# An encoder trunk on one core: the opening stage loads its one-hot table first, moves the bias-line products and re-deals the modulation sums

## The chip, the core and the metric

The kernel runs on one NeuronCore of a Trainium2 chip. TensorE (PE, with its weight loads as PEld) does matrix products, VectorE (DVE), ScalarE (ACT) and GpSimd (POOL) the elementwise work, and SyncE (SP) issues most of the DMA transfers; ACT and POOL can issue transfers too. Each engine works through its own instruction list in order and waits on semaphores for the others. The metric is the device time of one execution in microseconds (us), the median over several executions.

## What is computed

Two transformer layers over 1024 tokens of width 1024, fp32. Layer 0 is a dilated-window attention with a T5 bias by relative position, layer 1 a latent attention. Each layer first forms `u = x*(1+scale)+shift`, with `shift` and `scale` made from a conditioning vector:

```python
for i in range(DEPTH):
    mod = jax.nn.silu(c) @ ada_w[i] + ada_b[i]
    shift, scale, gate = jnp.split(mod[:, None, :], 3, axis=-1)
    u = x * (1 + scale) + shift
    ...
    x = layernorm(DEEPNORM_ALPHA * x + gate * y, ln_g[i], ln_b[i])
# in layer 0, per head: s = q.k/8 + bias_table[t5_bucket(distance)] inside the window
```

Only the opening of layer 0 is touched: the modulation (shift and scale), the first three output blocks of the input projection (q, k and v of the first head pair), and the lines of bias that all heads of layer 0 read.

## The kernel before

`startup` is the opening stage. Its order is written out by hand: every engine gets its instructions in the order of the Python calls. The contraction over 1024 channels is cut into eight slices `dd` of 128. For each slice it loads 1 MB of modulation weights (two tiles `ada`) and 512 KB of transposed input (`xc`), forms two columns (shift and scale for 128 channels), forms `u`, and adds the slice's share to six PSUM banks `ip`, two halves of 512 tokens for each of three weight blocks `wa`.

- **The columns.** `mod_acc(dd)` (L205-216) lets VectorE add up `SHARE[dd]` of the eight 128x256 weight pieces into `acc`, each scaled by a column of `sc` (the silu of the conditioning vector). `mod_sums(dd)` (L218-227) has TensorE sum the other pieces and `acc` over the partitions, with products of a single column into the bank `pm`: two per piece, each shown as two instructions in the profile. `mod_col(dd)` (L229-234) adds the bias columns `bcol` on ScalarE.
- **u in two parts.** fp32 products are done as three fp32r products of high and low parts. `u_hi` (L236-245) makes the high part `uh` (and the exact value back into `xc`), `u_lo` (L247-248) the low part `ul`. `w_split` (L102-106) does the same for weights: `wh` on ScalarE, `wl` here on VectorE.
- **The block.** `in_block(dd)` (L254-269) has 18 products of 512 columns, six for each weight block: `uh,wh`, `uh,wl` and `ul,wh` for two halves.
- **Zeros.** `zeros(n)` (L163-165) issues n products of 512 columns on a tile of zeros into a bank that nobody reads. They only keep TensorE occupied.
- **The bias lines.** `bias_load` loads the 32x18 table (`rb`, whose padding POOL fills) and the one-hot table `oh` (33 rows of 6 KB). `bias_line(g)` multiplies them, one product per head group, and ScalarE copies six rows to `lines`; `bias_write` stores these in DRAM, where `bias_tile` reads them per head.

In what order: the first slice's sums run with zeros between them, then the first block with the second slice's sums woven into it. From then on slice `dd`'s sums are issued, then the whole block of slice `dd-1`, so that the columns, `uh` and `ul` of `dd` are made during that block. The line products stand after the block of slice 5 (one) and after that of slice 6 (two, written at the start of `layer_a_attention` and moved there by the scheduler, which orders what follows the hand-written part); they are `pl` in the profile. Loads go out on SP in the order of the calls; every load takes one of eight semaphores in turn and waits until the load that had that semaphore eight loads earlier has landed. After `startup` come the projections (`pj`), layer 0's attention, and the rest, none of which the diff changes apart from the two line products at the start of `layer_a_attention`.

Of the kernel before, what the change touches and what calls it, by code (L numbers as in the profile page):

```python
# [34 lines left out]
SHARE = (4, 3, 5, 7, 7, 7, 7, 7)  # L35


ZEROS = (10, 6)
# [31 lines left out]
class Trunk:  # L70
# [85 lines left out]
    def startup(self):  # L156
# [13 lines left out]
        nc.scalar.dma_start(self.bcol1, A["ada_b1"])  # L170
        nc.scalar.activation(self.sc, self.sc, AF.Silu)
        self.rb = KP.tile([33, P], F32, name="rb")
        nc.gpsimd.memset(self.rb, NEG)
# [9 lines left out]
        def load_x(dd):  # L183
            t = self.gt(F32, "xc")
            sync.dma_start(t, A["xt"][dd])
            return t
# [16 lines left out]
        acc_psum = [[self.bank("ip") for _ in range(2)] for _ in range(3)]  # L203
        accs, pms = {}, {}

        def mod_acc(dd):
            w = [adas[dd][k // 4][:, (k % 4) * 256 : (k % 4) * 256 + 256] for k in range(8)]
            n = SHARE[dd]
            parts = [(w[k], self.sc[:, k : k + 1]) for k in range(8 - n)]
            if n:  # L210
                a = KP.tile([P, 256], F32, tag="ot", bufs=3, name=self.nm("acc"))
                nc.vector.tensor_scalar(a, w[8 - n], self.sc[:, 8 - n : 9 - n], None, op0=ALU.mult)
                for k in range(9 - n, 8):
                    nc.vector.scalar_tensor_tensor(a, w[k], self.sc[:, k : k + 1], a, op0=ALU.mult, op1=ALU.add)
                parts.append((a, self.ones))
            accs[dd] = parts

        def mod_sums(dd):  # L218
# [3 lines left out]
            for j in range(2):  # L222
                for i, (w, x) in enumerate(parts):
                    nc.tensor.matmul(
                        pm[:, j : j + 1], w[:, j * P : j * P + P], x, start=i == 0, stop=i == len(parts) - 1
                    )
                    yield 1.0
# [26 lines left out]
        def in_block(dd, blocks=(0, 1, 2)):  # L254
            for b in blocks:
                h, l = whl[b]
                ks = slice(dd * P, dd * P + P)
                hh, hl, lh = (h, self.uh[dd]), (h, self.ul[dd]), (l, self.uh[dd])
                if dd or b:
                    todo = [(x, hf) for x in (hh, lh, hl) for hf in range(2)]  # L260
                else:
                    todo = [(hh, 0), (hl, 0), (hh, 1), (lh, 0), (lh, 1), (hl, 1)]
                seen = set()
                for n, ((w, u), hf) in enumerate(todo):
                    nc.tensor.matmul(  # L265
                        acc_psum[b][hf], w[:, ks], u[:, hf * 512 : hf * 512 + 512],
                        start=dd == 0 and hf not in seen, stop=dd == NK - 1 and n >= 4,
                    )
                    seen.add(hf)
                    yield 1.0  # L270
# [17 lines left out]
        split(1)  # L288
        mod_acc(1)
        weave((in_block(0, (1,)), 6.0), (mod_sums(1), 12.0))  # L290
        split(2)
        for dd in range(1, NK):
            if dd + 2 < NK:
                load_d(dd + 2)
            if dd == 2:
# [1373 lines left out]
```

## Time and profile before

| | |
|---|---|
| timed runs, median of 3 | 1365.49 us (1363.44 to 1368.98) |
| the profiled execution | 1372.24 us, its span 1370.4 us |
| TensorE busy | 1339.2 us (98% of the span) |
| VectorE, ScalarE, GpSimd busy | 855.7, 798.4, 562.5 us |
| opening stage, up to the first projection product | 69.04 us |
| DMA from 10 to 40 us | 400 GB/s, all 16 engines taken |
| mean granted TensorE clock over the span | 0.987 |

The span is the time from the first to the last instruction of one profiled execution; 1.84 us of its own time lie around it. A view of stretches gives the busy time of each engine in a stretch (with the number of instructions), the granted clock as a share of full speed, and what the DMA engines moved. The chain of waits is followed back from the last instruction: each row has a start, a length and the work that held up the end. Rows of the timeline have start, length, engine, line, what is written and read, and in brackets how long the engine stood idle before it and for whom.

### The profile page before, as it was taken

What the parts mean: (1) busy time and instruction counts of PE and PEld (TensorE: products, weight loads), DVE (VectorE), ACT (ScalarE), POOL (GpSimd) and SP (SyncE); (2) the same over time, 40 slices, a digit from 0 to 9 for tenths busy, and PEclk for the clock granted to TensorE, in tenths of its full rate; (3) what the DMA queues carried; (4) which work ended last, traced back from release to release, by engine and by line L of the source; (5) the groups of instructions that cost most, each with busy time, mean ns of one, the idle gap of its engine ahead of it and who ended that gap; (6) DMA issues with size and microseconds to landing.
All of it is one profiled execution on the core that took longest, in us unless ns stands there. A gap on an engine that the chain in (4) does not pass through costs nothing.

```text
span 1370.4 us, 20504 instructions
## 1 busy us (share of the span) xinstructions
PE 1339.2 (98%) x7464; PEld 1152.6 (84%) x7464; DVE 855.7 (62%) x1473; ACT 798.4 (58%) x1631; POOL 562.5 (41%) x550
## 2 busy tenths in 40 slices
PE   8999999999999999999999999999999999999997
PEld 7788888888888888888988888898889889898776
DVE  5554454445445344566734278887887887777887
ACT  3575555554443432355742288788788878887421
POOL 0142233123222266614632344744553473444761
PEclk6999999999999999999999999999999999999998
DMA  9422221113244254552154011111112111113322
GB/s 361 109 66 37 60 62 40 37 48 99 85 143 152 64 158 136 186 175 115 62 143 153 0 34 30 24 41 25 30 27 54 30 24 28 25 55 118 114 93 92
DMA packets 44980, 114.28 MB, mean 83 GB/s; under 512 B 6917, under 2 KB 13333, under 8 KB 44880
## 3 DMA queue, kind: packets, MB, share of 16 engines
q1 hardware_dynamic: 40184, 100.43, 24.0%
q0 software_dynamic: 4096, 12.24, 3.6%
q8 instruction: 59, 0.97, 0.3%
q14 instruction: 41, 0.34, 0.1%
q10 hardware_dynamic: 600, 0.32, 0.1%
HBM read 96.42 MB, written 8.67 MB: 77 GB/s over the span
## 4 chain that ended last, share of the span: by engine, by line
PE 73%; DVE 10%; ACT 7%; DMA 5%; issue 4%; SPq 0%; POOL 0%; DVEq 0%; ACTq 0%; POOLq 0%
PE pj L92 8%; PE pj L94 8%; PE pj L93 8%; PE o L1388 6%; PE t L1368 5%; PE s L92 3%; PE s L94 3%; PE s L93 3%; DMA ada<-ada_row 3%; PE ip L265 3%; PE po L92 2%; PE po L94 2%; PE po L93 2%; DVE mb L1328 2%; PE t L564 2%
## 5 line engine op out<-in xcount | busy, mean ns | idle before, releaser
L92 PE MATMUL pj<-uh,wh 128*128 128x512 f32 x528 | 217.5, 412 | 0.0
L94 PE MATMUL pj<-uh,wl 128*128 128x512 f32 x528 | 207.5, 393 | 0.0
L93 PE MATMUL pj<-ul,wh 128*128 128x512 f32 x528 | 207.3, 393 | 0.0
L1328 DVE TENSOR_REDUCE mb<-s 128x1 f32<-128x1024 f32 x128 | 155.6, 1216 | 48.8 <-PE s L94 47.9
L1372 DVE TENSOR_TENSOR ptl<-t,pth 128x512 fp32r<-128x512 f32 x256 | 165.0, 680 | 5.3 <-ACT pth L1371 3.2
L1371 ACT CAST pth<-t 128x512 fp32r<-128x512 f32 x256 | 139.4, 589 | 37.8 <-PE t L1368 34.4
L105 POOL TENSOR_TENSOR wl<-wraw,wh 128x1024 fp32r<-128x1024 f32 x42 | 106.2, 2533 | 123.0 <-ACT wh L104 93.2
L1336 ACT ACTIVATE pr<-s,mb 128x1024 f32<-128x1024 f32 x128 | 144.2, 1126 | 15.1 <-DVE mb L1328 14.5
L1368 PEld LDWEIGHTS t<-ident,pr 128*128 128x128 f32 x1024 | 119.3, 141 | 19.0 <-DVE ptl L1372 2.8
L1368 PE MATMUL t<-ident,pr 128*128 128x128 f32 x1024 | 133.0, 272 | 2.1 <-DVE ptl L1372 2.1
L1388 PE MATMUL o<-pth,vq 128*128 128x256 f32 x512 | 130.4, 292 | 1.1 <-DVE ptl L1372 1.1
L1388 PE MATMUL o<-ptl,vq 128*128 128x256 f32 x512 | 125.5, 283 | 2.0 <-DVE ptl L1372 1.8
L553 ACT ACTIVATE sb<-sb,stat 128x256 f32<-128x256 f32 (+1 forms) x144 | 67.0, 466 | 95.2 <-DVE stat L547 95.1
L94 PEld LDWEIGHTS pj<-uh,wl 128*128 128x128 f32 x528 | 99.4, 188 | 22.3
L1399 POOL TENSOR_TENSOR osum<-osum 64x256 f32<-64x256 f32 x64 | 47.7, 746 | 163.5 <-ACT osum L1398 162.3
L93 PEld LDWEIGHTS pj<-ul,wh 128*128 128x128 f32 x528 | 100.1, 190 | 14.0
L92 PEld LDWEIGHTS pj<-uh,wh 128*128 128x128 f32 x528 | 99.9, 189 | 14.2
L92 PE MATMUL s<-kb,q 128*128 128x512 f32 x256 | 105.8, 413 | 0.1
L94 PE MATMUL s<-kb,q 128*128 128x512 f32 x256 | 100.4, 392 | 0.0
L93 PE MATMUL s<-kb,q 128*128 128x512 f32 x256 | 100.4, 392 | 0.0
L1388 PEld LDWEIGHTS o<-ptl,vq 128*128 128x128 f32 x512 | 97.8, 191 | 3.0 <-DVE ptl L1372 3.0
L1388 PEld LDWEIGHTS o<-pth,vq 128*128 128x128 f32 x512 | 97.5, 191 | 1.7 <-DVE ptl L1372 1.6
(289 smaller groups left out, 3151.2 us busy)
## 6 DMA issues: line engine op xcount, KB each, us to landing
wraw<-wa SPq DMA_DIRECT2D x36, 512.0 KB
ada<-ada_row SPq DMA_DIRECT2D x64, 256.0 KB
wraw<-wo_a SPq DMA_DIRECT2D x18, 512.0 KB
ada<-ada_ss SPq DMA_DIRECT2D x16, 512.0 KB
kb<-kb POOLq DMA_DIRECT2D x30, 256.0 KB, 4.6
f<-f_d SPq DMA_DIRECT2D x18, 256.0 KB
xc<-xt SPq DMA_DIRECT2D x8, 512.0 KB
xr<-x SPq DMA_DIRECT2D x8, 512.0 KB
```

The lines of the kernel that those rows point to most:

```text
L92: mm(out, wh, xh, start=start, stop=False)
L93: mm(out, wh, xl, start=False, stop=False)
L94: mm(out, wl, xh, start=False, stop=stop)
L105: (lo_engine or self.nc.gpsimd).tensor_tensor(l[:, :width], raw[:, :width], f32(h[:, :width]), op=ALU.subtract)
L553: nc.scalar.activation(sb[:, a * w : a * w + w], sb[:, a * w : a * w + w], AF.Exp, bias=stat[:, 0, hh, t : t + 1], scale=-1.0, accum_out=s ...
L1328: nc.vector.tensor_reduce(m[:, 0:1], s, axis=AX.X, op=ALU.max, negate=True)
L1336: nc.scalar.activation(pr, s, AF.Exp, bias=m[:, 0:1], accum_out=dens[u // 8][:, u % 8 : u % 8 + 1])
L1368: nc.tensor.transpose(pt[:, c * P : c * P + P], pr[:, kt * P : kt * P + P], self.ident)
L1371: nc.scalar.copy(h, src)
L1372: nc.vector.tensor_tensor(l, src, f32(h), op=ALU.subtract)
L1388: nc.tensor.matmul(po[:, 0:256], v, pts[j][x][:, c * 256 : c * 256 + 256], start=n == 0, stop=n == 15)
L1399: nc.gpsimd.tensor_tensor(w3[mine, 0:256], w3[mine, 256:512], w3[mine, 0:256], op=ALU.add)
```

## The change

- **Loads.** The one-hot table is the first transfer on SP. The bias table is now built on the host with its padding (33x128) and is the second transfer of ScalarE's queue, between the conditioning vector and the bias columns. The first weight block comes before the first slice's `xc`, which is loaded in two halves; the third weight block comes before the second slice's `xc`.
- **Line products.** The three stand behind the first ten zeros, with their copies on ScalarE; the writes to DRAM are issued by GpSimd after the first block.
- **Single-column sums.** `SHARE` gives VectorE 7, 5, 7 pieces of the first three slices where it had 4, 3, 5, always the first ones; a piece's two columns follow each other.
- **Order.** The sums of slice `dd+1` are one run inside block `dd`, after eight of its 18 products; in blocks 1 to 6 the six `ul` products come last. In the first slice's block the sums of slice 1 run beside the third weight block. The banks `ip` are taken when first used. Zeros are 10, 2, 4 and 4 (with four among the first sums, they were 10, 4 and 6 and one more).

```diff
-SHARE = (4, 3, 5, 7, 7, 7, 7, 7)
-ZEROS = (10, 6)
+SHARE = (7, 5, 7, 7, 7, 7, 7, 7)
+ZEROS = (10, 2, 4, 4)
...
-        zeros(ZEROS[0])
-        nc.scalar.dma_start(self.sc, A["c"])
-        nc.scalar.dma_start(self.bcol, A["ada_b0"])
...
+        self.bias_load()
...
-        load_d(0)
+        adas[0] = load_ada(0)
+        nc.scalar.dma_start(self.bcol, A["ada_b0"])
...
         raws[0] = self.w_load(A["wa"][0])
+        xcs[0] = load_x(0, HALVES)
+        raws[1] = self.w_load(A["wa"][1])
         adas[1] = load_ada(1)
-        raws[1] = self.w_load(A["wa"][1])
+        raws[2] = self.w_load(A["wa"][2])
         xcs[1] = load_x(1)
-        raws[2] = self.w_load(A["wa"][2])
         load_d(2)
...
         def in_block(dd, blocks=(0, 1, 2)):
...
+            if 0 < dd < NK - 1:
+                todo.sort(key=lambda t: t[1] >= 4)
...
-        mod_acc(0)
-        for n, _ in enumerate(mod_sums(0)):
-            if n % 2:
-                zeros(1)
+        zeros(ZEROS[0])
+        mod_acc(0)
+        for g in range(3):
+            self.bias_line(g)
+        nc.vector.tensor_scalar(self.bcol[:, :, 1], self.bcol[:, :, 1], 1.0, None, op0=ALU.add)
         zeros(ZEROS[1])
+        all_of(mod_sums(0))
+        zeros(ZEROS[2])
+        split(0)
         mod_col(0)
         u_hi(0, HALVES[0])
         u_lo(0, HALVES[0])
-        split(0)
         u_hi(0, HALVES[1])
         u_lo(0, HALVES[1])
         all_of(in_block(0, (0,)))
         split(1)
+        all_of(in_block(0, (1,)))
         mod_acc(1)
-        weave((in_block(0, (1,)), 6.0), (mod_sums(1), 12.0))
         split(2)
+        sums, third = mod_sums(1), in_block(0, (2,))
+        weave((steps(sums, 6), 6.0), (steps(third, 4), 4.0))
+        all_of(sums)
+        zeros(ZEROS[3])
+        all_of(third)
+        for g in range(3):
+            self.bias_write(g)
         for dd in range(1, NK):
...
-            if dd > 1:
-                all_of(mod_sums(dd))
             mod_col(dd)
             u_hi(dd)
             if dd + 1 < NK:
                 mod_acc(dd + 1)
             u_lo(dd)
-            all_of(in_block(dd - 1, (2,) if dd == 1 else (0, 1, 2)))
-            if dd == 6:
-                self.bias_line(0)
-        self.bias_write(0)
-        all_of(in_block(NK - 1))
+            block = in_block(dd)
+            if dd + 1 < NK:
+                all_of(steps(block, 8))
+                all_of(mod_sums(dd + 1))
+            all_of(block)
...
     def bias_write(self, g):
-        (self.nc.scalar if g else self.nc.sync).dma_start(self.lines_d[g], ...)
+        self.nc.gpsimd.dma_start(self.lines_d[g], self.lines[32 * g : 32 * g + 6, :])
...
     def layer_a_attention(self):
-        for g in (1, 2):
-            self.bias_line(g)
-            self.bias_write(g)
```

TensorE's list from the start to the first products of the first block, before (`pz` zeros, `pm` the single-column sums, `ip` the block's banks):

```order
L165 MATMUL pz_88<-zeros_86 128x512 x10
L224 MATMUL pm_142<-sc,ada_105 128x1 x2
L165 MATMUL pz_88<-zeros_86 128x512
L224 MATMUL pm_142<-sc,ada_105 128x1 x2
L165 MATMUL pz_88<-zeros_86 128x512
L224 MATMUL pm_142<-ones,acc_137 128x1
...
L165 MATMUL pz_88<-zeros_86 128x512 x7
L265 MATMUL ip_130<-uh_166,wh_171 128x512
L265 MATMUL ip_130<-ul_167,wh_171 128x512
```

and now (`pl` is a line product):

```order
L165 MATMUL pz_88<-zeros_86 128x512 x10
L348 MATMUL pl_145<-oh,rb 128x512
L348 MATMUL pl_148<-oh,rb 128x512
L348 MATMUL pl_151<-oh,rb 128x512
L165 MATMUL pz_88<-zeros_86 128x512 x2
L220 MATMUL pm_157<-sc,ada_99 128x1 x2
L220 MATMUL pm_157<-ones,acc_137 128x1 x2
L165 MATMUL pz_88<-zeros_86 128x512 x4
L272 MATMUL ip_180<-uh_172,wh_166 128x512
L272 MATMUL ip_180<-uh_172,wl_167 128x512
```

Ten single-column products became four and stand in one run, and the line products stand between them and the first zeros.

ScalarE's list in the same place, before and then now:

```order
L168 DMA sc<-c 128x8
L169 DMA bcol<-ada_b 128x16
L170 DMA bcol_81<-ada_b 128x32
L171 ACT_TABLE_LOAD
L171 ACTIVATE sc<-sc 128x8
L232 ACTIVATE mcol<-pm_142,bcol 128x1 x2
L241 ACTIVATE uh_166<-xc_109,mcol 128x512
L104 ACTIVATE wh_171<-wraw_111 128x1024
L241 ACTIVATE uh_166<-xc_109,mcol 128x512
```

```order
L337 DMA sc<-c 128x8
L338 DMA rb<-rel_bias 33x128
L187 DMA bcol<-ada_b 128x16
L188 DMA bcol_81<-ada_b 128x32
L189 ACT_TABLE_LOAD
L189 ACTIVATE sc<-sc 128x8
L354 COPY lines<-pl_145 6x512
L354 COPY lines<-pl_148 6x512
L354 COPY lines<-pl_151 6x512
L104 ACTIVATE wh_166<-wraw_105 128x1024
L229 ACTIVATE mcol<-pm_157,bcol 128x1 x2
L238 ACTIVATE uh_172<-xc_107,mcol 128x512 x2
```

Three copies and the first weight split now stand ahead of the first columns on ScalarE.

TensorE's list of the second slice's block, now (before, the 18 products stood together, and the next slice's sums ahead of all of them):

```order
L272 MATMUL ip_192<-uh_242,wh_188 128x512
L272 MATMUL ip_193<-uh_242,wh_188 128x512
L272 MATMUL ip_192<-uh_242,wl_189 128x512
L272 MATMUL ip_193<-uh_242,wl_189 128x512
L220 MATMUL pm_263<-sc,ada_121 128x1 x2
L220 MATMUL pm_263<-ones,acc_246 128x1 x2
L272 MATMUL ip_212<-uh_242,wh_206 128x512
L272 MATMUL ip_213<-uh_242,wh_206 128x512
L272 MATMUL ip_212<-uh_242,wl_207 128x512
L272 MATMUL ip_213<-uh_242,wl_207 128x512
L272 MATMUL ip_180<-ul_243,wh_166 128x512
L272 MATMUL ip_181<-ul_243,wh_166 128x512
```

The sums of the next slice (`pm_263`) have moved from ahead of this slice's 18 products to behind eight of them.

More of the change, by code (lines that the diff above doesn't have):

```diff
@@ L181, in load_ada, with load_x @@
             return t
-        def load_x(dd):
+        def load_x(dd, parts=(slice(0, 1024),)):
             t = self.gt(F32, "xc")
-            sync.dma_start(t, A["xt"][dd])
+            for sl in parts:
+                sync.dma_start(t[:, sl], A["xt"][dd][:, sl])
             return t
@@ L202, in startup @@
         self.uh, self.ul = [None] * NK, [None] * NK
-        acc_psum = [[self.bank("ip") for _ in range(2)] for _ in range(3)]
+        acc_psum = [None] * 3
         accs, pms = {}, {}
@@ L208, in mod_acc @@
             n = SHARE[dd]
[L209 to L216, printed above, removed]
+            a = KP.tile([P, 256], F32, tag="ot", bufs=3, name=self.nm("acc"))
+            nc.vector.tensor_scalar(a, w[0], self.sc[:, 0:1], None, op0=ALU.mult)
+            for k in range(1, n):
+                nc.vector.scalar_tensor_tensor(a, w[k], self.sc[:, k : k + 1], a, op0=ALU.mult, op1=ALU.add)
+            accs[dd] = [(w[k], self.sc[:, k : k + 1]) for k in range(n, 8)] + [(a, self.ones)]
         def mod_sums(dd):
@@ L1631, in _arrays @@
     a["wa"] = c(np.concatenate([w[0:3].transpose(1, 0, 2, 3).reshape(27, P, 1024), w[3]]))
-    a["rel_bias"] = c(I["rel_bias"])
+    rel = np.full((33, 4, 32), NEG, np.float32)
+    rel[:32, :3, :6] = I["rel_bias"].reshape(32, 3, 6)
+    a["rel_bias"] = rel.reshape(33, P)
     a["ident"] = np.eye(P, dtype=np.float32)
```

66 lines of the change are left out of this document (33 added, 33 removed).

## The prediction

> **What bounds the kernel now.** First, three stretches of the span (busy time of each engine, granted clock, DMA share, GB/s):
>
> ```profile
> core 0: us, PE busy (x) PEld busy (x) DVE busy (x) ACT busy (x) POOL busy (x), PEclk, DMA share, GB/s
> 10.00:40.00 30.00, 29.86 (x115) 25.36 (x116) 18.02 (x31) 13.06 (x19) 0.00 (x0) 0.64 1.03 400
> 40.00:69.04 29.04, 29.04 (x136) 22.47 (x135) 17.09 (x29) 17.22 (x26) 5.15 (x15) 1.00 0.29 52
> 69.04:1370.40 1301.36, 1274.32 (x7194) 1100.08 (x7192) 817.91 (x1407) 766.60 (x1586) 555.74 (x524) 1.00 0.26 75
> ```
>
> TensorE is busy nearly always, so a stage is worth what TensorE is spared in it. After 69.04 us its clock is full and the diff changes nothing: that part will only shift. Between 10 and 40 us the granted clock is 0.64 on average, and there the opening loses most. The chain of waits (start, length, work) in the opening:
>
> ```profile
> 1.18 6.07 DMA bcol<-ada_b
> ...
> 9.42 0.98 PE pm L224 x4
> ...
> 15.91 1.91 ACT wh L104 x2
> ...
> 29.75 6.86 PE ip L265 x18
> ...
> 51.69 0.79 PE pm L224 x8
> 52.48 4.25 PE ip L265 x18
> 56.72 1.05 PE pl L341 x2
> ...
> 62.99 1.91 PE pl L341 x4
> ```
>
> So the first sums wait for VectorE's `acc`, and that for the bias columns' transfer, which VectorE's list names ahead of it. After 29.75 TensorE alone carries the chain: blocks of 18 products, sums, line products. The timeline of TensorE dates the steps:
>
> ```profile
> 9.42 0.56 PE L224 MATMUL pm<-ones,acc 128*128 128x1 f32 x2 [2.48 <-DVE acc L214]
> ...
> 15.96 0.63 PE L265 MATMUL ip<-uh,wh 128*128 128x512 f32 x1
> ...
> 29.61 1.20 PE L265 MATMUL ip<-uh,wh 128*128 128x512 f32 x2
> ...
> 69.04 0.39 PE L92 MATMUL pj<-uh,wh 128*128 128x512 f32 x1
> ```
>
> The first block starts at 15.96, the second slice's block at 29.61, the projections at 69.04. Why the clock is low shows in stretches of 3.41 us; its changes (near 7.94, 18.18, 21.58, 35.24) lie whole multiples of that apart. All instructions, in five of these stretches:
>
> ```profile
> 4.53:7.94 3.41, 2.42 (x14) 1.72 (x13) 0.63 (x3) 0.21 (x1) 0.00 (x0) 1.00 1.01 377
> 18.18:21.58 3.40, 3.26 (x23) 2.96 (x23) 3.33 (x6) 0.00 (x0) 0.00 (x0) 1.00 1.04 404
> 21.58:25.00 3.42, 3.42 (x13) 3.04 (x13) 2.09 (x5) 1.15 (x3) 0.00 (x0) 0.50 1.02 407
> 25.00:28.41 3.41, 3.41 (x15) 3.05 (x13) 1.57 (x3) 1.74 (x2) 0.00 (x0) 0.50 1.05 338
> 31.83:35.24 3.41, 3.41 (x9) 2.64 (x8) 2.39 (x4) 0.92 (x1) 0.00 (x0) 0.50 1.03 412
> ```
>
> Those of the banks `ip` alone, in the second of them and in one later:
>
> ```profile
> 18.18:21.58 3.40, 2.30 (x7) 0.92 (x6) 0.00 (x0) 0.00 (x0) 1.00 1.04 404
> 62.55:65.96 3.41, 1.57 (x7) 0.97 (x7) 0.00 (x0) 0.00 (x0) 1.00 0.99 82
> ```
>
> The single columns alone in the former, and the line products alone in the latter:
>
> ```profile
> 18.18:21.58 3.40, 2.16 (x16) 2.68 (x17) 0.00 (x0) 1.00 1.04 404
> ```
>
> ```profile
> 62.55:65.96 3.41, 1.98 (x4) 0.67 (x4) 1.15 (x2) 1.00 0.99 82
> ```
>
> From 18.18 to 21.58 TensorE was busy almost throughout, yet the clock was then halved for four stretches: 16 of its instructions were single columns and seven were wide. From 62.55 to 65.96 there were also seven wide ones, with four line products beside them, and the clock stayed. So by these rows single columns do not hold the clock, wide and line products do; the stretch before the half clock ended (31.83 to 35.24) held nine wide products and nothing else.
>
> **The change part by part**, costed in the profiled execution's own time.
>
> *The first block's start.* ScalarE's rows for what stands ahead of it (start, length), then VectorE's, then SP's issues and one of SP's waits:
>
> ```profile
> 5.06 0.21 ACT L171 ACTIVATE sc<-sc 128x8 f32<-128x8 f32 x1 [1.64 <-DMA sc<-c]
> ...
> 13.45 0.81 ACT L241 ACTIVATE uh<-xc,mcol 128x512 fp32r<-128x512 f32 x1
> ...
> 52.96 1.25 ACT L241 ACTIVATE uh<-xc,mcol 128x1024 fp32r<-128x1024 f32 x1
> ...
> 57.81 0.57 ACT L343 COPY lines<-pl 6x512 f32<-6x512 f32 x1 [2.33 <-PE pl L341]
> 58.80 0.41 ACT L232 ACTIVATE mcol<-pm,bcol 128x1 f32<-128x1 f32 x2 [0.41 <-PE pm L224]
> ```
>
> ```profile
> 15.49 1.22 DVE L105 TENSOR_TENSOR wl<-wraw,wh 128x1024 fp32r<-128x1024 f32 x1
> 16.62 0.54 DVE L245 TENSOR_SCALAR xc<-xc,mcol 128x512 f32<-128x512 f32 x1
> 17.20 0.69 DVE L248 TENSOR_TENSOR ul<-xc,uh 128x512 fp32r<-128x512 f32 x1
> ...
> 28.33 3.09 DVE L214 SCALAR_TENSOR_TENSOR acc<-ada,sc,acc 128x256 f32<-128x256 f32 x6
> ```
>
> ```profile
> 9.71 0.33 SPq L185 DMA_DIRECT2D xc<-xt  x1
> ...
> 16.39 1.61 SPq L180 DMA_DIRECT2D ada<-ada_ss  x2
> ```
>
> ```profile
> SPq L185 <- DMA wraw<-wa: 0.3, 1, 0.3
> ```
>
> The bias table's landing is not in the trace in this place. From below it cannot precede `sc`, ahead of it in ScalarE's queue (5.06); from above, the second load of that queue before, with 128 rows, landed at 7.25 (chain, 1.18 + 6.07). With 33 rows I take a quarter of the way, 5.7. Three line products at 1.91/2 end by 8.6. The copies (0.57) follow one by one, the last to 9.3; the first weight split (1.91/2) to 10.3; two columns (0.41) to 10.7; half of `uh` (0.81) to 11.5. First block at 11.6, where it was 15.96. VectorE's `acc` of seven pieces (3.09/6 each, 3.6), no longer behind the bias columns, starts when the first modulation weights are there (about 6.1, below) and ends at 9.7: the sums behind the second zeros (9.1) wait 0.6 us, still ahead of ScalarE's 10.3. Weights: the wait before SP's issue at 9.71 was for the first block's weights, then the fourth 512 KB load, and the ninth landed by the issue at 16.39, so a load takes 1.34 us. As third, behind the 0.2 MB table (0.9 us, see below), they land at 9.3, just when ScalarE's list comes to them; the first load of all, 9.71 - 3 x 1.34 = 5.7 at the latest, moves to 6.6 at most; `sc` allows a start at 5.06; I take 6.1.
>
> The table's price: 0.2 MB at 400 GB/s are 0.5 us, and the stretch from 25.00 to 28.41, in which it ran before, moved 338 GB/s against 407 in the one ahead, 0.6 us lost; so 0.5 to 1.1, and I take 0.9, below the upper end, since the small bias table was loaded in that stretch too.
> The Trainium skill, "DMA: Bandwidth & Descriptors", section "Why a DMA increments its semaphore by 16 and not by 1", says that a transfer runs on the largest number of engines up to 16 that divides its rows. The table's 33 rows would have 11, 0.7 us as an estimate at that share of 400 GB/s; this speaks against heading the queue with it, and the trace's loss agrees in direction.
>
> *The second block's start.* VectorE has: `wl` 1.22 to 11.5, then per half 0.54 + 0.69 (to 14.1), `wl` of block 1 to 15.3, five pieces of `acc` 2.6 to 17.9, `wl` of block 2 to 19.1. The third weights, now the eighth load and not the ninth, land at 16.39 - 1.34 + 0.9 = 15.9, their `wh` ends at 16.9. TensorE: blocks 0 and 1, held by VectorE, to 15.8; four products and six single columns (0.79/4 each) to 19.0; two columns of `acc` to 19.4. ScalarE: 0.41 + 1.25 to 21.1, while zeros and the last two products fill TensorE. Slice 1's block: 21.1 for 29.61, **-8.5**.
>
> *The rest of the opening.* From 29.61 to 69.04 are 39.43 us. Now it is seven blocks of 4.25 and six sets of sums of 0.79: 34.5, **-4.9**. That is the three line products, -2.96, the half clock up to 35.24, -2.8, and one set of sums more, +0.79. The sums in mid-block need `acc` (VectorE has 3.6 + 1.2 = 4.8 us of work for each 5.04 us) and feed ScalarE: 0.41 + 1.25 + about 0.25 of gaps = 1.9 us, covered by ten products, 10 x 4.25/18 = 2.4. The cover is 0.5 us; were it gone, six blocks would each pay what is missing.
>
> *At nothing.* The DRAM writes of the lines go to POOL, which is idle:
>
> ```profile
> 62.85 2.38 POOL L105 TENSOR_TENSOR wl<-wraw,wh 128x1024 fp32r<-128x1024 f32 x1 [60.61 <-ACT wh L104]
> ```
>
> They are issued near 20 us and read after 50. Later loads are not late: slice 2's last is the twelfth, near 21.2, and a slice's three loads take 4.0 us where TensorE takes 5.04. Were they late, each block would wait for them. Eight banks suffice: zeros, six `ip` and one `pm`, the lines' three being copied by 9.3.
>
> *Sum:* -8.5 - 4.9 = -13.4 on 1372.24 (its span of 1370.4 and 1.84 around it), that is 1358.8. This execution is 6.75 us above the median. Two readings: had the clock not fallen the second time, 21.58 to 35.24 would have cost half, -6.8, just the median, and then the timed runs already have part of my gain and 1358.8 stands; or profiling adds 6.75 everywhere and 1365.49 - 13.4 = 1352.1. The spread of the timed runs (5.5 us) is like one more or less halving, so I weigh the first more: **1357 us**.
>
> **Rivals.** *The clock falls again.* Between the third zeros' end (10.7) and 16.9 TensorE has gaps of about a microsecond at both ends and only 12 wide products between. Stretches of 3.41 us placed as in this trace hold about eight of them (more than the seven that stayed with lines beside them), but their phase differs between executions and a stretch from 10.7 to 14.1 would hold five. Then the next stretch or two run at half: some 3.5 us of products once more, 1362. For it: the fall after 7.94 came with only 2.48 us of idle. Against: far fewer single columns, four and eight for ten and twelve.
> By the Trainium skill, "TensorE: Matmul & The Clock Gate", section "Part 1: The HAM clock gate", the clock falls after an idle window of about 3.4 us; a gap of 1.1 us could not do it, and the sum stays 1358.8. The trace disagrees in part: it fell after stretches with 1.0 us of idle (4.53 to 7.94) and 0.14 us (18.18 to 21.58).
>
> *The change doesn't hide what it says.* If ScalarE's 1.9 us come out as 3.0 beside the second `xc` activation, six blocks wait 0.6 us each: 3.6 back from 1357, 1360.6. For it: the cover is only 0.5. Against: ScalarE has 0.41 + 2 x 1.25 = 2.9 us of work in 5.04.
>
> *Slower.* SP's fifth to ninth loads now wait for small loads of ScalarE's queue that hold their semaphores. If the fat table delays these, SP stops and the whole stream moves. Before, they landed between 5.06 and 9; each microsecond beyond 9 moves every later slice by one. The loads issued ahead of them (1.8 MB) keep the engines busy to about 9. From 7 us of standstill on (bias columns at 16) the median is passed; at 15 us it would be 1373. Nothing in the trace is near that: the same loads ran beside a full stream.
>
> **How the numbers follow.** Forecast 0.60, its own range 1351 to 1361; clock 0.22; cover 0.08; slower 0.05; a rest of 0.05 for more gain than either reading. The range reaches from the second reading to the clock's rival, 1351 to 1364. A measurement of this kernel tells 0.5% (6.8 us) from no change, so faster means under 1358.7: 0.70 of the forecast (0.42), 0.15 of the clock's rival (0.03), a quarter of the cover's (0.02) and the rest (0.05) give 0.52; slower 0.05; the same 0.43.
>
> **What would show it.** The first block near 11.6, slice 1's block near 21.1, TensorE's eighteen products of the last slice done near 55.6, blocks 5.04 us apart without idle, the clock 1.00 from about 5 us on. Wrong if: a 0.50 stretch after 10 us (clock), TensorE waiting on `uh` before each block (cover), idle DMA engines before 12 us (slower). If the lines start after 7 us, the first block's term is too large by as much.

## The result, and the profile after

| | before | after |
|---|---|---|
| median | 1365.25 us (1362.94 to 1368.98) | 1356.85 us (1354.89 to 1360.80) |
| ratio of the two, 95% interval | | 0.9943 (0.9925 to 0.9960) |
| profiled execution, its span | 1372.24, 1370.4 us | 1356.85, 1355.1 us |
| mean granted clock over the span | 0.987 | 0.994 |

The change makes the kernel 0.57% faster, 8.4 us between the medians. To split the two spans at the same piece of work, I take a product of the first attention scores that follows the opening in both kernels with the same instructions behind it (7125 on TensorE): the third group of `s<-k,qh`. It starts at 84.03 us before and 72.34 after. Three stretches of the span, the last one the part behind that product; after:

```profile
core 0: us, PE busy (x) PEld busy (x) DVE busy (x) ACT busy (x) POOL busy (x), PEclk, DMA share, GB/s
10.00:40.00 30.00, 29.52 (x144) 24.44 (x145) 26.58 (x47) 16.36 (x24) 0.00 (x0) 0.91 1.03 409
40.00:72.34 32.34, 30.37 (x149) 24.71 (x148) 19.22 (x37) 23.54 (x40) 14.46 (x31) 1.00 0.27 76
72.34:1355.10 1282.76, 1260.28 (x7125) 1088.95 (x7123) 806.05 (x1388) 755.56 (x1563) 547.54 (x507) 1.00 0.26 76
```

and before:

```profile
84.03:1370.40 1286.37, 1260.48 (x7125) 1088.89 (x7123) 809.43 (x1388) 755.04 (x1563) 546.52 (x507) 1.00 0.26 75
```

So of the 15.3 us between the spans 11.7 are gone ahead of that product and 3.6 behind it, in work that the change does not touch. TensorE does 144 instructions between 10 and 40 us where it did 115, at a granted clock of 0.91 and not 0.64.

The timeline of TensorE after, at the steps that the prediction dated:

```profile
1.58 4.22 PE L165 MATMUL pz<-zeros 128*128 128x512 f32 x10 [1.58 <-DVE zeros L160]
5.73 2.84 PE L348 MATMUL pl<-oh,rb 33*128 33x512 f32 x6
...
9.47 0.85 PE L220 MATMUL pm<-sc,ada 128*128 128x1 f32 x4
10.18 0.99 PE L220 MATMUL pm<-ones,acc 128*128 128x1 f32 x4
11.03 2.05 PE L165 MATMUL pz<-zeros 128*128 128x512 f32 x4
12.88 0.63 PE L272 MATMUL ip<-uh,wh 128*128 128x512 f32 x1
...
19.45 0.58 PE L220 MATMUL pm<-ones,acc 128*128 128x1 f32 x4
...
21.82 0.73 PE L272 MATMUL ip<-uh,wh 128*128 128x512 f32 x2 [0.29 <-ACT uh L238]
...
26.98 0.62 PE L272 MATMUL ip<-uh,wh 128*128 128x512 f32 x2
...
52.15 0.61 PE L272 MATMUL ip<-uh,wh 128*128 128x512 f32 x2
...
53.88 0.50 PE L92 MATMUL pj<-uh,wh 128*128 128x512 f32 x1 [0.66 <-ACT wh L104]
...
72.34 0.28 PE L550 MATMUL s<-k,qh 128*128 128x256 f32 x1
```

The line products fill 5.73 to 8.6. The first block starts at 12.88 (15.96 before), slice 1's block at 21.82 (29.61), and from 26.98 to 52.15 five blocks follow each other in 5.03 us each without a wait. Two projection products have slipped into the last block and wait 0.66 us there for their split weights.

ScalarE's timeline after shows what stood ahead of the first block:

```profile
8.60 0.58 ACT L354 COPY lines<-pl 6x512 f32<-6x512 f32 x1 [0.28 <-PE pl L348]
9.60 1.06 ACT L104 ACTIVATE wh<-wraw 128x1024 fp32r<-128x1024 f32 x1 [0.41 <-DMA wraw<-wa]
11.21 0.41 ACT L229 ACTIVATE mcol<-pm,bcol 128x1 f32<-128x1 f32 x2 [0.56 <-PE pm L220]
11.65 1.52 ACT L238 ACTIVATE uh<-xc,mcol 128x512 fp32r<-128x512 f32 x2
```

The clock in stretches of about 3.41 us, after:

```profile
5.38:8.79 3.41, 3.41 (x9) 1.34 (x8) 2.27 (x5) 1.34 (x3) 0.90 (x2) 0.97 0.99 357
8.79:12.20 3.41, 3.41 (x13) 3.03 (x13) 2.33 (x5) 2.41 (x5) 0.89 (x2) 0.50 1.04 419
12.20:15.60 3.40, 3.40 (x10) 2.32 (x9) 3.03 (x5) 1.92 (x3) 0.00 (x0) 0.53 1.03 413
15.60:19.00 3.40, 3.21 (x21) 2.72 (x19) 3.26 (x7) 1.06 (x1) 0.00 (x0) 1.00 1.03 415
```

TensorE was busy through the whole first stretch, most of it with line products, and the clock halved 0.2 us before its end, at 8.58, for two stretches, until 15.40. In the opening it fell once; in that of before it fell twice.

### The profile page after: what moved, and what is told of

The parts are those of the page before. It is cut to its first block, busy times and chain, and to the rows that moved or that the text cites. A ratio compares the mean times of both kernels' runs of the same rounds, so it can differ in the third digit from the quotient of the medians.

```text
span 1355.1 us, 20458 instructions
## 1 busy us (share of the span) xinstructions
PE 1328.6 (98%) x7435; PEld 1143.5 (84%) x7435; DVE 855.9 (63%) x1480; ACT 799.1 (59%) x1631; POOL 565.3 (42%) x552
## 4 chain that ended last, share of the span: by engine, by line
PE 78%; DVE 7%; ACT 7%; DMA 3%; issue 3%; SPq 0%; ACTq 0%; DVEq 0%
PE pj L92 8%; PE pj L94 8%; PE pj L93 8%; PE o L1396 6%; PE t L1376 5%; PE po L92 4%; PE po L93 4%; PE po L94 4%; PE s L92 3%; PE s L94 3%; PE s L93 3%; PE pg L92 2%; PE pg L93 2%; PE pg L94 2%; PE ip L272 2%
## 5 line engine op out<-in xcount | busy, mean ns | idle before, releaser
L1344 ACT ACTIVATE pr<-s,mb 128x1024 f32<-128x1024 f32 x128 | 144.2, 1126 | 15.4 <-DVE mb L1336 14.7
```

What stands on the lines that cost most here:

```text
L1344: nc.scalar.activation(pr, s, AF.Exp, bias=m[:, 0:1], accum_out=dens[u // 8][:, u % 8 : u % 8 + 1])
```

## The experiments

All runs in one table. The ratio is to runs of the kernel before on the same chip beside each; the last four columns are from the profile of each (us): the start of the first block, of slice 1's block, of the third group of `s<-k,qh` (the mark), and the time from the mark to the end.

| kernel | median | ratio (95% interval) | first block | slice 1 | mark | behind it |
|---|---|---|---|---|---|---|
| before | 1365.25 | | 15.96 | 29.61 | 84.03 | 1286.4 |
| before_again | 1365.68, one time | | 15.46 | 25.33 | 79.09 | 1284.7 |
| after | 1356.85 | 0.9943 (0.9925 to 0.9960) | 12.88 | 21.82 | 72.34 | 1282.8 |
| after_again | 1358.10 | 0.9941 (0.9920 to 0.9961) | 12.81 | 22.18 | 72.72 | 1281.3 |
| lines_late | 1362.50 | 0.9974 (0.9960 to 0.9987) | 11.46 | 20.64 | 75.67 | 1285.2 |
| lines_zeros | 1360.84 | 0.9962 (0.9943 to 0.9981) | 13.19 | 21.96 | 72.50 | 1285.8 |
| sums_late | 1369.32 | 1.0016 (0.9999 to 1.0033) | 12.85 | 21.68 | 85.95 | 1283.2 |
| share_old | 1362.81 | 0.9982 (0.9965 to 0.9998) | 15.43 | 25.52 | 76.94 | 1284.4 |
| acc_late | 1358.71 | 0.9944 (0.9926 to 0.9962) | 15.28 | 24.51 | 75.05 | 1282.0 |
| zeros33 | 1360.01, one time | | 15.91 | 25.44 | 75.96 | 1282.2 |
| w2_early | 1357.63 | 0.9930 (0.9915 to 0.9945) | 12.80 | 22.07 | 72.60 | 1283.7 |
| sums_first | 1357.29 | 0.9932 (0.9915 to 0.9949) | 12.81 | 21.71 | 72.23 | 1284.6 |
| combo | 1356.08 | 0.9923 (0.9906 to 0.9941) | 12.88 | 20.89 | 71.96 | 1281.9 |
| stacked | 1356.91 | 0.9930 (0.9910 to 0.9949) | 12.00 | 20.39 | 71.46 | 1282.7 |

### The two kernels once more: which reading of the profiled execution holds

No edit; before_again is the kernel before, after_again the changed kernel.

> The kernel before, unchanged, in one more profiled execution. Theory: the 6.75 us between its first profiled execution (1372.24) and the median come from where the clock's stretches of 3.41 us fall. Then this execution's opening ends (first projection product) well before 69.04 if its time is near 1365, by about the same difference, and half-clock stretches outside the opening (466 to 469 us there) need not come again. Rival: the opening always ends near 69.04 and the difference lies elsewhere.

> The changed kernel once more, as the measure for the others of this chip. Theory P (the opening alone carries the gain; the rest of the difference between the two profiles is where stretches of half clock happened to lie): median near 1356.9, and in the profile the first block near 12.9, slice 1's block near 21.8 and the opening's last product near 57.2, each within 1.7 us (half a stretch of 3.41 us at half clock), with the part behind the opening between 1297 and 1300. Rival O (the new order also changes something behind the opening): the part behind the opening comes out at 1297.9 again, with no fall of the clock near 460 us, while the kernel before shows one each time.

Two of the same stretches of before_again, and its first block and its mark in the timeline:

```profile
10.00:40.00 30.00, 29.64 (x140) 24.68 (x140) 22.23 (x39) 16.00 (x23) 0.00 (x0) 0.83 1.03 396
79.09:1363.80 1284.71, 1260.17 (x7125) 1088.93 (x7123) 809.08 (x1388) 755.26 (x1563) 545.06 (x507) 1.00 0.26 75
```

```profile
15.46 0.63 PE L265 MATMUL ip<-uh,wh 128*128 128x512 f32 x1
...
79.09 0.28 PE L539 MATMUL s<-k,qh 128*128 128x256 f32 x1
```

The same program reached the mark 4.9 us sooner than in the first profile, with a clock of 0.83 between 10 and 40 us and not 0.64: it was at half speed for shorter times. This shows in the timed runs too, since each lists its mean granted clock. Of 54 runs of the kernel before that stood beside the experiments, 26 had 0.988 to 0.992 and took 1368.65 us in the mean, 24 had 0.993 or 0.994 and took 1364.4 (the other four, at 0.995 to 0.997, took 1363.1 to 1366.2). So the time of the kernel before goes with its clock, 4.3 us between the two means, and the first profile, 1372.24 at 0.987, lay beyond the longest of these runs (1371.83). In the changed kernel's own 13 runs this does not hold: the four above 1360 us had 0.995 to 0.997, the nine below 1358.2 had 0.993 to 0.996. What made those four longer no trace shows.

The part behind the mark takes between 1281.3 and 1286.4 us over all fourteen profiles, in no order by what their openings do. The first profile's clock also fell once, from 465.3 to 468.7 us (about 1.7 of the 3.6 us above); it fell in that region in lines_late, share_old and sums_first too, which have the new order, and not in before_again. The two profiles of before are the higher there by 3.5 us in the mean of two each; lines_late and lines_zeros lie among them, share_old and sums_first just below. I take it for chance, but two profiles of each cannot exclude a microsecond or two. In the frame of after_again's expectation its part behind the opening is 1296.4 (1354.0 less 57.6), 0.6 below the range of theory P; rival O falls with before_again, which has no fall near 460 us.

### The place of the line products

```diff
 # lines_late: nothing behind the first zeros, no write behind the first block; in the loop over slices
+            if dd == NK - 1:
+                for g in range(3):
+                    self.bias_line(g)
+                    self.bias_write(g)
 # lines_zeros: two zeros behind each line product, none in one run (ZEROS 10, 0, 4, 4)
         for g in range(3):
             self.bias_line(g)
+            zeros(2)
```

> The changed kernel with the three line products, their copies and writes put ahead of the last slice's block; the table is still loaded first. Theory: the early place costs nothing (the first weight split waits for its load until 9.6 us anyway), so putting them back costs their 2.9 us: the opening ends at 60 instead of 57.2 and the median is 2.9 above the change's. Rival: the early place costs the clock (it fell at 8.79 after a stretch full of line products); then the first block starts earlier than 12.88, at about 12, and the net loss is 2 us or less.

> The changed kernel with two zeros behind each line product (and none behind the last one besides). Theory: line products (33 rows) hardly count for the clock and wide products do. Then the clock does not fall near 8.8, the sums and the first block run at full speed, the first block starts near 12.0 instead of 12.88, and the opening ends 0.5 to 1.5 us earlier. Rival: the clock falls there for another reason, or line products count as much as wide ones: then nothing changes in the clock and the opening ends within 0.5 us of 57.2.

Without the lines the first block starts at 11.46, where the prediction had put it for the changed kernel, and slice 1's block 1.2 to 1.5 us sooner than in it; the lines then cost 2.9 us late in the opening, at full clock. TensorE of lines_late:

```profile
11.46 0.79 PE L272 MATMUL ip<-uh,wh 128*128 128x512 f32 x1
...
51.08 2.91 PE L348 MATMUL pl<-oh,rb 33*128 33x512 f32 x6
```

So at slice 1's block the early place gives back about half of the lines' time: 2.9 late against 1.2 to 1.5 early. At the first scores even less is left, 0.5 to 0.9 us (62.19 for 61.29 and 61.66), since the wait of 0.66 us in the last block is gone as well. So far the rival of the expectation holds. By its ratio this part of the change is worth more, some 4 us, and the mark agrees with the ratio: 75.67 for 72.34 and 72.72. The time is lost between the first scores and the mark, where TensorE stands idle and the clock falls behind it, from 72.1 to 75.5, as in no profile of the changed kernel:

```profile
72.27 1.18 PE L575 MATMUL t<-ident,sb 128*128 128x128 f32 x4 [2.43 <-ACT sb L564]
```

The wait is 2.43 us and not 1.09 as in after_again and in before. ScalarE and VectorE are late there behind a weight split that began at 67.51, after 5.86 us of idle ScalarE, where after_again's began at 61.23. In SP's list six transfers of bias lines waited for the late write, and the next three weights were issued behind them, from 58.02 us on (from 44.47 in after_again). The trace does not name what the split waited for; that the late weights held it is likely. The kernel before had its first line written earlier (bias lines from 59.85 on, scores at 73.12; here 55.09 and 62.19), so the 4 us are the price of this late place and not of the old one, which no run brings back.

lines_zeros moved the fall of the clock one stretch on, from 8.6 to 11.7, made it one stretch long and not two, and gained nothing by it: first block 13.19, where its theory had 12.0, slice 1's block 21.96, mark 72.50. Its ratio is 0.2% the higher, but its interval overlaps that of the changed kernel. So a fall one stretch later brought nothing here, with four zeros more in TensorE's list.

### The height of a product and the clock

```diff
-                nc.tensor.matmul(pz, zt[:, 0:P], zt[:, P : P + 512], start=True, stop=True)
+                nc.tensor.matmul(pz, zt[0:33, 0:P], zt[0:33, P : P + 512], start=True, stop=True)
```

> All zero products are done on 33 rows and not on 128, which is the height of the line products; nothing that enters the output changes. Theory R (the clock counts how much of the array a product uses, so products of 33 rows hardly hold or raise it): the clock is 0.50 at 5 us and up to the end of a stretch filled with the first and second block (14 us or later), the line products take twice as long or the same 2.84 us for three pairs, and the first block starts 0.3 to 1.5 us later than 12.9. Theory W (width alone counts, 512 columns, and the fall at 8.8 us came from the idle time between the lines and the sums): the clock goes to 1.00 near 5 us and falls near 8.8 as in the changed kernel.

TensorE of zeros33, and two of its stretches:

```profile
6.01 5.32 PE L348 MATMUL pl<-oh,rb 33*128 33x512 f32 x6
...
15.91 0.79 PE L272 MATMUL ip<-uh,wh 128*128 128x512 f32 x1
...
19.48 1.05 PE L272 MATMUL ip<-ul,wh 128*128 128x512 f32 x2
20.34 0.72 PE L272 MATMUL ip<-uh,wl 128*128 128x512 f32 x2
```

```profile
5.00:8.40 3.40, 3.40 (x6) 1.70 (x6) 2.17 (x5) 0.45 (x1) 0.00 (x0) 1.00 1.02 389
15.20:18.60 3.40, 3.40 (x8) 2.16 (x8) 3.22 (x5) 2.68 (x4) 0.00 (x0) 1.00 1.03 413
```

With all zeros on 33 rows the six instructions of the line products take 5.32 us where they took 2.84, and the block's pairs take 1.05 until about 20.3 and 0.72 from there. So products on 33 rows, back to back from 1.58 to 12.1 us, do not bring TensorE to full speed; the first blocks, on 128 rows, do, after some 4.4 us of them. Theory R holds, and was too cheap: the first block starts 3.1 us later than in after_again, the mark lies 3.2 us later.

The granted clock in these rows is 1.00 all the while: here the column shows full speed where no change was recorded. At the start of a program speed is read from durations, not from that column. By the Trainium skill, "TensorE: Matmul & The Clock Gate", section "Part 1: The HAM clock gate", TensorE starts at half rate and activity releases it; the durations agree, 0.89 us for an instruction of a line product here against 0.47 in the changed kernel.

Whether line products count for nothing is another question. The stretch ahead of the fall in after held 2.84 us of them and 0.71 of zeros on 128 rows. In lines_zeros the clock stayed after a stretch with 2.06 of lines and 1.56 of zeros (4.85 to 8.26), and fell after one with 1.30 of lines, 1.67 of zeros and 0.95 of single columns (8.26 to 11.67). The zeros alone would order these two the other way round, so a line product seems to count for something, and for less than one on 128 rows; no run settles how much.

### The shares, and VectorE's order

```diff
 # share_old
-SHARE = (7, 5, 7, 7, 7, 7, 7, 7)
+SHARE = (4, 3, 5, 7, 7, 7, 7, 7)
 # acc_late
+        nc.vector.tensor_scalar(self.bcol[:, :, 1], self.bcol[:, :, 1], 1.0, None, op0=ALU.add)
         mod_acc(0)
         for g in range(3):
             self.bias_line(g)
-        nc.vector.tensor_scalar(self.bcol[:, :, 1], self.bcol[:, :, 1], 1.0, None, op0=ALU.add)
```

> Only the shares go back: VectorE sums 4, 3 and 5 of the eight pieces for the first three slices and not 7, 5 and 7, so TensorE does 6, 4 and 4 single columns more (two instructions each, 0.12 us each at full clock, 0.25 at half). Theory F (fewer columns are worth their own time): the first block starts 0.8 us later than in the changed kernel, slice 1's block 1.0 to 1.8 later, slice 2's another 0.5; median 1.5 to 2.5 above the changed kernel's. Rival C (single columns cost above all by the clock): the stretch they fill brings a second fall between 17 and 25 us, and the opening ends 3.5 us or more later. Rival N: the longer accumulation on VectorE eats the gain, and slice 1's block starts within 0.3 us of 22.0.

> Only VectorE's order goes back: the addition on the bias columns stands ahead of the first accumulation again, all else as in the changed kernel. Theory W (that wait was worth removing): the bias columns land near 8.4, the accumulation starts near 8.6 where it started at 5.8 and ends near 12.2, the first block starts 1.5 to 2.5 us later than 12.85, near 14.9, and slice 1's block as much later, since VectorE's work stands in a row from there: median 1.5 to 2.5 above the changed kernel's. Rival N (the chain is held by ScalarE's copies and the first weights anyway): the first block within 0.5 us, no change.

TensorE of share_old, then VectorE of acc_late:

```profile
9.46 3.41 PE L220 MATMUL pm<-sc,ada 128*128 128x1 f32 x16
...
15.43 0.63 PE L272 MATMUL ip<-uh,wh 128*128 128x512 f32 x1
```

```profile
8.87 0.17 DVE L282 TENSOR_SCALAR bcol<-bcol 128x8 f32<-128x8 f32 x1 [7.27 <-DMA bcol<-ada_b]
8.96 0.35 DVE L209 TENSOR_SCALAR acc<-ada,sc 128x256 f32<-128x256 f32 x1
9.35 3.09 DVE L211 SCALAR_TENSOR_TENSOR acc<-ada,sc,acc 128x256 f32<-128x256 f32 x6
```

Either part alone, when it is undone, puts the first block back to 15.3 or 15.4, about where it was before (15.46 and 15.96). Theory F of share_old had the chain, but at 0.8 us for the first block where 2.6 were measured. They are two chains to the same columns, and the later one counts: in share_old TensorE's columns (16 instructions at half clock, 3.41 us), in acc_late VectorE's wait for the bias columns. So their worths do not add up. There is no second fall in share_old (rival C), but the first half-clock time lasted until about 19.3, a stretch longer; its mark is 4.2 us later than in after_again, its ratio 0.4% higher, 5.6 us. For acc_late the trace shows 2.3 us at the mark and the ratio shows nothing; an interval of 0.18% to each side (2.5 us) can hide them, and I leave open whether they are all lost in the mean over executions.

### The place of the next slice's sums

```diff
-                all_of(steps(block, 8))
+                all_of(steps(block, 16))
```

> The changed kernel with the next slice's sums behind 16 of a block's 18 products instead of 8. Theory: the mid-block place hides 1.9 us of ScalarE's work (two columns and uh) behind ten products; behind two (0.46 us) 1.4 us of it are open in each of six blocks, +8 to +9 us, with TensorE waiting for uh at each block's start. Rival: ScalarE's work is short of the path or the clock's falls dominate: less than 3 us.

TensorE of sums_late, the first of six such waits:

```profile
28.16 0.72 PE L272 MATMUL ip<-uh,wh 128*128 128x512 f32 x2 [1.20 <-ACT uh L238]
```

All its products on `ip` from slice 1 on, grouped, with what they waited for (us, times), and two stretches of its clock:

```profile
  ACT uh L238: 7.5, 7
```

```profile
40.00:50.00 10.00, 8.46 (x37) 6.48 (x36) 6.41 (x13) 3.74 (x7) 0.00 (x0) 0.83 0.39 88
60.00:70.00 10.00, 7.78 (x30) 5.75 (x29) 2.60 (x3) 5.21 (x8) 3.78 (x12) 0.83 0.14 41
```

With two products behind the sums and not ten, six blocks wait 1.20 us each: ScalarE's two columns and `uh` are no longer covered. That is 7.2 us of the 13.2 by which the mark is later than in after_again. In that time the clock fell three times more (29.0 to 32.5, and 0.83 in each of the two stretches above, which is 3.4 us at half speed in ten), some 1.7 us each, 5.1; the remaining microsecond is not traced. The median is 11.2 us above after_again's, by the ratio 10.

This is the price of a place that is too late. It is not what the mid-block place gained over the kernel before: there the sums stood ahead of the block before theirs, all 18 products covered ScalarE, and the blocks followed each other in 5.04 us as well:

```profile
41.46 0.28 PE L224 MATMUL pm<-sc,ada 128*128 128x1 f32 x2
...
46.50 0.28 PE L224 MATMUL pm<-sc,ada 128*128 128x1 f32 x2
```

No run puts the sums back to that place, so what it is worth stays open, as it does for the order of the loads.

### What holds slice 1's block, and a kernel that should be faster

```diff
 # w2_early: third weights ahead of the second modulation weights
-        adas[1] = load_ada(1)
         raws[2] = self.w_load(A["wa"][2])
+        adas[1] = load_ada(1)
 # sums_first
-        weave((steps(sums, 6), 6.0), (steps(third, 4), 4.0))
+        weave((steps(sums, 6), 6.0), (steps(third, 2), 2.0))
 # combo: w2_early, no weave (all sums ahead of the third block), ZEROS 10, 2, 4, 2, and in the loop
+            if dd == NK - 1:
+                self.a_ready[3] = self.w_split(self.a_queue.pop(3))
             mod_col(dd)
 # stacked: combo, ZEROS 10, 10, 4, 2, and one line product on 128 rows (tables built so on the host)
-        for g in range(3):
-            self.bias_line(g)
+        self.bias_line()
```

> The third weights are loaded ahead of the second modulation weights. Theory T (slice 1's block waits for the transfer of the third weights, whose split began at 16.27 behind 2.15 us of waiting): they land 2 x 1.34 us earlier, the split ends near 15.3, and slice 1's block starts up to 1.1 us sooner, 20.7, median 1355.8. Theory V (it waits for VectorE's accumulation, 16.01 to 18.44 in the changed kernel, and for the single columns woven between the third block's products): the split's wait goes, slice 1's block stays within 0.3 us of 21.8, median within 0.5 us of the changed kernel's.

> The six single columns of slice 1 are woven with two and not four of the third block's products, so that the accumulated columns come two products (1.0 us) sooner; all else as in the changed kernel. Theory V (slice 1's block waits for the chain of single columns, columns to ScalarE and uh): the accumulated columns end near 18.8 where they ended at 20.03, uh's slice 1 ends near 20.5, and the block starts when four products and four zeros are done, near 20.9 for 21.8: median 0.9 us below the changed kernel's. Theory T (the transfer of the third weights sets it): slice 1's block at 21.8 as before, and no gain.

> Meant to beat the changed kernel: the third weights ahead of the second modulation weights; all of slice 1's single columns ahead of the third block (no weave) with two zeros for four; the split of the first projection weights ahead of the last slice's columns on ScalarE. By the chain of columns (theory V): slice 1's sums end near 19.2 where they ended at 20.0 to 20.4, its block starts near 21.0 (changed kernel 21.8 and 22.2), the wait of 0.66 us in the last block goes, the opening ends 1.8 us sooner, median 1356.2 beside 1358.1. Rival: the 16 column instructions and few wide products in one stretch bring another fall of the clock behind 20 us, as one did after 18.18 to 21.58 in the kernel before; then 1.7 us of it are lost again.

> As the one with all columns ahead of the third block and the early split, and the three line products are one: the one-hot table's three parts are stacked on 99 of 128 rows, the bias table stands in blocks beside them with zeros elsewhere, so one product gives the three groups' lines and ScalarE copies them at once; the second zeros are ten, not two. Theory R (products of 33 rows do not hold the clock, and the copies stand ahead of the first split on ScalarE): the lines take 0.9 us and not 2.9, the clock stays 1.00 through 8 to 17 us, the first split starts near 9.5, the first block near 11.9 (12.85), slice 1's block near 20.0, median another 1.0 to 1.5 below the former, 1355. Rival: the first weights and VectorE's row of work set the first blocks, and both come no sooner: the clock stays at 1.00, but slice 1's block stays near 21, and the median within 0.4 us of the former's.

The transfer does not hold slice 1's block: with w2_early the split no longer waits for the third weights, and the block starts at 22.07 for 22.18 in after_again, whose half clock lies in nearly the same place. The sums do in part: 0.47 us sooner than there in sums_first (21.71), about half of what I expected. In combo the block comes at 20.89, as expected, and the clock does not fall again; but TensorE waits for VectorE at the sums, and the gain at the last block turns into a new wait at the first scores:

```profile
18.48 0.61 PE L220 MATMUL pm<-ones,acc 128*128 128x1 f32 x4 [0.17 <-DVE acc L211]
...
20.89 0.71 PE L272 MATMUL ip<-uh,wh 128*128 128x512 f32 x2
...
60.12 0.36 PE L550 MATMUL s<-k,qh 128*128 128x256 f32 x1 [0.61 <-DVE k L442]
```

In stacked the clock holds, and VectorE's row of work is what is left. The column alone would not show it, but the durations do (ten zeros in 2.87 us from 6.99 on, the four single-column instructions on `ada` in 0.50 where the changed kernel's took 0.85):

```profile
8.40:11.80 3.40, 3.30 (x19) 2.51 (x17) 2.38 (x5) 2.14 (x4) 1.77 (x3) 1.00 1.04 405
11.80:15.20 3.40, 2.52 (x8) 1.39 (x9) 3.15 (x5) 2.75 (x4) 0.00 (x0) 1.00 1.03 413
```

```profile
12.00 0.49 PE L272 MATMUL ip<-uh,wh 128*128 128x512 f32 x1 [0.30 <-ACT uh L238]
...
14.50 0.50 PE L272 MATMUL ip<-ul,wh 128*128 128x512 f32 x1 [0.68 <-DVE ul L245]
...
20.39 0.71 PE L272 MATMUL ip<-uh,wh 128*128 128x512 f32 x2
```

No half clock is left between 7 and 40 us, a third of the line work is, the first block starts at 12.00, and yet slice 1's block comes only 0.5 us before combo's: VectorE is busy 3.15 us of 3.40. The clock and the first block came as its theory said, slice 1's block between the theory's 20.0 and the rival's 21, and the median did not fall, as the rival said. Both kernels have the lowest marks, 71.96 and 71.46, but their ratios overlap that of the changed kernel, so that neither is shown to be faster than it; combo's six runs lie closest together, 1355.2 to 1356.61.

## Why the prediction was right, step by step

The predicted 1357.0 met 1356.85. It rested on a sum of -13.4 us in the frame of the profiled execution and on a choice between two readings.

- **The sum, -13.4: measured -11.7 at the mark.** *The first block at 11.6: 12.88.* Three terms are short. The first weights were not there "just when ScalarE's list comes to them" but 0.41 us later. The columns waited 0.56 us for the sums, and the four zeros ahead of the block, 2.05 us long, held it to 12.88, although the first half of `uh` was done at about 12.4: both ran at half clock. *Slice 1's block at 21.1: 21.82.* Only 0.7 of the 1.3 us came through, since the sum itself let TensorE wait from 15.8 to 16.9 for the third weights' split; that split ended at 17.33, the sums at 20.03 where the sum had 19.4. *The rest of the opening, 34.5: 35.4*, from 21.82 to 57.2 (the last block's end at 57.66 less 0.46 for the two projection products inside it). Five of the blocks took 5.03 as predicted (5.04); 0.66 is the wait for the projection weights' split, which the sum did not have.
- **"Single columns do not hold the clock, wide and line products do": wrong of the line products.** They are wide but 33 rows high. The stretch that they filled ended in half clock, and zeros33 shows that such products do not raise the clock either. The step read from 62.55 to 65.96 had seven wide products of 128 rows beside the four on lines, so it could show that lines add something, but not that they hold the clock alone. That is the term that was mis-sized: the sum had no half clock behind 5 us, and there were two stretches of it, 6.8 us, from 8.58 to 15.40.
- **The clock's rival, 1362: its condition came true, its price did not.** "Wrong if: a 0.50 stretch after 10 us" was seen, to 15.40. It was priced at 3.5 us of products once more; the steps above put it at about 1 us at the first block and 0.7 with the rest at slice 1's block. The likely reason is that the blocks of slice 0 are held by VectorE, which the prediction said: in stacked, at full clock, TensorE waits 0.68 us for `ul` in the first block, and lines_zeros and stacked, whose clocks fell later or not at all, moved slice 1's block little.
- **The two readings, and luck.** The first reading is the better one: the first profiled execution stood at a long phase of half clock, and "the timed runs already have part of my gain" agrees with the 54 runs. In before_again's phase the mark moves by 6.4 to 6.8 us and in the first profile's by 11.3 to 11.7; the 8.4 between the medians lie between. The second reading (profiling adds 6.75 everywhere) is wrong: the profiled executions of before_again and of the changed kernel took 1365.68 and 1356.85, close to the medians. That the forecast met the number within 0.15 us is in part luck. By the first reading alone it would have been 1358.8, from a gain too large by 1.7; with the 11.7 that the mark shows it would have been 1360.5, and the 3.6 us behind the mark, which no term of the sum had, make up the rest. The 1.8 us that were taken off for the second reading stood in their place.
- **The cover.** 0.5 us was estimated. No block waits, and sums_late, which takes eight of the ten covering products away, has 1.20 of wait in each. Eight products last 8 x 4.25/18 = 1.9 us, so the cover was 1.9 - 1.2 = 0.7.
- **SP's waits (slower).** Not seen: the DMA share was 0.99 to 1.04 from 5.4 to 19 us. *At nothing* held for the late loads: no block waits for a transfer after 17.4. The lines' writes went out from 7.77 us on, not near 20, and nothing waited for them.

## What to carry to other kernels

Before a gain is added up from one profiled execution, look at what that execution's clock did: here the same program reached the same product 4.9 us apart, and a change that shortens the uncertain stage also takes away some of that. A short run of sums that another engine turns into the next block's input needs more products behind it than the conversion lasts. Where several chains lead to the same start, undo each part alone: here each of two parts, taken back by itself, lost nearly the whole early start. And a part that is moved to a third place, as the lines and the sums were here, shows the price of that place and not what the change gained.

## What the runs showed of the hardware

- Products on 33 rows did not raise TensorE's clock (10 zeros and 6 line instructions in a row, 10 us, in zeros33); 4.2 us of zeros on 128 rows did (after). A stretch of 3.41 us with 2.84 us of them and 0.71 of 128-row zeros ended in half clock, one with 2.06 and 1.56 did not (lines_zeros). How many rows are enough was not tried.
- In zeros33 and stacked, where no change was recorded in the opening, the granted clock reads 1.00 throughout, also where durations show half speed (zeros33, up to 20.3 us).
- Among 50 runs of one and the same kernel, the 26 with a mean granted clock of 0.992 or less took 4.3 us longer in the mean than the 24 with 0.993 or 0.994.
